# A mixture-of-experts stream written in a fixed engine order, and a hinted branch ahead of it

## The chip, the cores and the metric

The kernel runs on one core of a Trainium2 chip, in one launch. The metric is the device time of one execution in microseconds, as the median of several runs. TensorE multiplies (PE, its weight loads PEld), VectorE (DVE) and ScalarE (ACT) work beside it, SyncE (SP) holds the queue that issues the weight transfers, GpSimd (POOL) does little here.

## The reference, cut to what matters

The program is two transformer blocks on 256 tokens of width 1024, in float32: sliding-window attention, a feed-forward layer, a second attention, then a mixture of experts, and a second block of a recurrent and an attention mixer, memory attention and a feed-forward layer. The change is in the mixture of experts: each token goes to 2 of 8 experts.

```python
def _moe(x, router, w_gate, w_up, w_down):
    ...
    vals, ids = lax.top_k(logits, TOP_K)
    w = jax.nn.softmax(vals, axis=-1)
    gate = jnp.sum(jax.nn.one_hot(ids, N_EXPERTS, dtype=jnp.float32) * w[..., None], axis=1)
    out = jnp.zeros_like(xt)
    for e in range(N_EXPERTS):
        out = out + gate[:, e:e + 1].astype(xt.dtype) * _swiglu(xt, w_gate[e], w_up[e], w_down[e])
    return out.reshape(B, S, D)
```

An expert is `(silu(x @ w_gate) * (x @ w_up)) @ w_down` with a hidden width of 3584, so its three weights are 1024 x 3584, 1024 x 3584 and 3584 x 1024.

## The kernel before, in words

**Products.** Every float32 product is made of three: each operand is split into a high part in TensorE's short float32 and a low part, the rest. `gemm` (L260) multiplies high by high, high by low and low by high (L274 to L276) into one PSUM tile. Weights come in pieces of 256 rows by 512 columns, 512 KB each. `fetch` (L207) issues the transfer on SyncE's queue into one of 9 raw buffers (`NRAW`), `split_w` (L241) casts the piece to its high part on ScalarE (L256) and subtracts for the low part on VectorE (L257), into one of 5 pairs of split buffers (`NSPL`). A piece feeds six matmuls of 512 columns.

**Experts.** `moe` (L983) routes the tokens, gives each expert 128 slots and gathers its tokens into them by a product with a one-hot matrix (L1102); the tokens come two experts at a time. For each expert there are seven chunks of 512 hidden columns. A chunk is a gate product of 4 pieces (24 matmuls), the silu on ScalarE (L1162), an up product of 4 pieces, a multiplication on VectorE (L1170), and four transposes of the result on TensorE (L186), whose copy to a high part is ScalarE's (L189) and whose low part is VectorE's (L190). Then come two down products of 14 pieces, one for each half of the output columns; each is scaled by the gates (L1179, L1180) and scattered back to the tokens by a product with the transposed one-hot matrix (L1084, L1085) and added (L1087).

**Order.** The code is written product by product: the pieces of a product are loaded one by one where they are used, a gather is written where its part of the tokens is first read, and the transposes and the scatter right behind their product. That is not the order in which the engines run it. A scheduler takes the instructions when the program is built, ranks them by their place in the text and by its own estimate of when each is ready, and writes one fixed queue for each engine. What stands in a queue waits for what stands ahead of it. PSUM has four buffers for products and gathers (`mm`), two for transposes (`tr`), two for scatters (`at`).

**Slots from 128 on.** An expert can have more than 128 tokens. The largest count is read into a register on each engine (L1130), and a branch (L1131) goes past `moe_rest`, which would work on the slots from 128 on with a slower product. With these inputs the branch goes past it. Ahead of it 14 pieces are loaded (5 of them split, L1120), and the last four megabytes of weights of the last expert are parked in buffers of their own (L1153).

```python
full = nc.values_load(cnti[0:1, 0:1], min_val=0, max_val=T)
with tc.If(full > P):
    for e in range(NE):
        self.moe_rest(p, p2, onehots, scatter, e, Xh, Xl)
```

Of the kernel before, what the change touches and what calls it, by code (L numbers as in the profile page):

```python
# [8 lines left out]
F32 = mybir.dt.float32  # L9
# [89 lines left out]
class Net:  # L99
# [513 lines left out]
    def ffn_body(self, Wg, g0, Wu, u0, dff, Wd, emit, scale=None, beside=lambda p: None):  # L613
# [369 lines left out]
    def moe(self):  # L983
# [5 lines left out]
        with ExitStack() as c0:  # L989
# [103 lines left out]
            def gather(oh):  # L1093

                xg = [p.tile([P, KD, 2, P], F32R, tag=f"xg{n}", name="xg") for n in "hl"]

                def bring(k0):
                    for X, x in zip((Xh, Xl), xg):
                        ps = self.mm.tile([P, 2, 2, P], F32, tag="mm", name="mm")
                        for k in range(2):  # L1100
                            for tt in range(2):
                                nc.tensor.matmul(ps[:, k].rearrange("p a s -> p (a s)"), X[tt][:, (k0 + k) * P:(k0 + k + 1) * P],  # L1102
                                                 oh[:, tt].rearrange("p a s -> p (a s)"), start=tt == 0, stop=tt == 1)
# [5 lines left out]
                there = set()  # L1109
# [36 lines left out]
            for e0 in range(0, NE, 2):  # L1146
                oh, back = onehots((e0, e0 + 1), 0)
                brought = gather(oh)
                if e0 == 0:

                    last = [self.xp.tile([P, 4, 512], F32, tag="xh", name="parked"), *(p.tile([P, 4, 512], F32, name=f"parked{n}") for n in range(3))]
# [919 lines left out]
```

## Time and profile before

| what | us |
|---|---|
| median of 3 runs | 2371.4 (2370.0 to 2378.3) |
| the profiled execution, its own time | 2368.11 |
| its span, first to last instruction | 2366.3 |
| before the first gather of the experts | 601.76 |
| from there to the end of the last expert's last product | 1009.46 |
| from there to the end | 755.08 |
| TensorE busy, of the span | 2261.2 |
| VectorE, ScalarE busy | 1778.9, 1440.7 |

The profile is of one execution. Busy time of TensorE is modelled: a matmul is shown from its start to the end of its passage, which overlaps the next, so a stretch can be fully busy and still hold gaps between starts. An arrow in a row points from an instruction to what ended the idle time before it, or from a waiting engine to what it waited for. L12 is line 12 of the kernel; a name with q (PEq, SPq) is the engine's sequencer, which waits, branches and issues transfers.

### The profile page before, as it was taken

How to read it: one execution, taken by the hardware profiler on the slowest of the kernel's cores; microseconds unless marked ns; L12 is line 12 of the kernel's file. 1: busy time of each engine (PE TensorE's matmuls, PEld its weight loads, DVE VectorE, ACT ScalarE, POOL GpSimd, SP SyncE). 2: the span in 40 equal slices, each digit the busy share in tenths (PEclk: the TensorE clock that was granted, in tenths of full speed). 3: DMA queues.
4: the chain of work that ended last, by engine and by line, in shares of the span. 5: the costliest groups of instructions: out<-in, count | busy, mean ns of one | idle time of the engine just before them, and what ended most of it. 6: DMA issues, size and time to landing. Idle time of an engine off the chain costs nothing.

```text
span 2366.3 us, 35741 instructions
## 1 busy us (share of the span) xinstructions
PE 2261.2 (96%) x12969; PEld 1923.0 (81%) x12969; DVE 1778.9 (75%) x2849; ACT 1440.7 (61%) x2386; POOL 66.1 (3%) x78
## 2 busy tenths in 40 slices
PE   8999998999899999999999999996898999989998
PEld 6699977887787787778777877775898888988997
DVE  7765559766788988889888888887857765666664
ACT  5664436665677767777777777774553554455553
POOL 0000000000000000000000000001110110000000
PEclk9999999999899999999999999998998999999999
DMA  8366555434899999999999999994333213543761
GB/s 242 98 198 192 187 160 175 148 107 145 289 364 350 350 350 345 357 352 343 346 365 349 358 334 357 355 323 132 108 90 99 74 54 110 170 143 137 260 200 46
DMA packets 319711, 541.96 MB, mean 229 GB/s; under 512 B 21839, under 2 KB 95015, under 8 KB 319271
## 3 DMA queue, kind: packets, MB, share of 16 engines
q1 hardware_dynamic: 309680, 528.93, 66.6%
q10 hardware_dynamic: 9847, 10.67, 1.5%
q8 instruction: 104, 1.70, 0.3%
q14 instruction: 80, 0.66, 0.1%
HBM read 536.38 MB, written 3.15 MB: 228 GB/s over the span
## 4 chain that ended last, share of the span: by engine, by line
PE 65%; DVE 4%; issue 3%; ACT 1%; POOL 1%; DMA 0%; DVEq 0%; POOLq 0%; ACTq 0%
PE mm L275 15%; PE mm L276 15%; PE mm L274 15%; PE tr L186 2%; PE mm L688 1%; PE mm L318 1%; PE mm L689 1%; PE mm L687 1%; PE mm L319 1%; PE mm L317 1%; PE tr L1701 1%; DVE wl L254 1%; PE at L1712 1%; PE at L1715 1%; PE mm L1102 1%
## 5 line engine op out<-in xcount | busy, mean ns | idle before, releaser
L257 DVE TENSOR_TENSOR wl<-w,wh 128x1024 fp32r<-128x1024 f32 x755 | 884.4, 1219 | 171.9 <-ACT wh L256 166.9
L256 ACT CAST wh<-w 128x1024 fp32r<-128x1024 f32 x755 | 753.9, 1050 | 179.3 <-PE mm L276 114.2
L275 PE MATMUL mm<-wl,xg 128*128 128x512 f32 x896 | 364.8, 407 | 0.6
L276 PE MATMUL mm<-wh,xg 128*128 128x512 f32 x896 | 351.4, 392 | 0.0
L274 PE MATMUL mm<-wh,xg 128*128 128x512 f32 x896 | 349.7, 392 | 0.0
L253 ACT CAST wh<-w 128x512 fp32r<-128x512 f32 (+1 forms) x378 | 216.3, 616 | 135.5 <-PE mm L276 59.6
L254 DVE TENSOR_TENSOR wl<-w,wh 128x512 fp32r<-128x512 f32 (+1 forms) x378 | 247.1, 682 | 52.0 <-ACT wh L253 51.5
L275 PEld LDWEIGHTS mm<-wl,xg 128*128 128x128 f32 x896 | 168.4, 188 | 65.8 <-DVE wl L257 35.7
L274 PEld LDWEIGHTS mm<-wh,xg 128*128 128x128 f32 x896 | 168.2, 188 | 36.0
L276 PEld LDWEIGHTS mm<-wh,xg 128*128 128x128 f32 x896 | 168.8, 188 | 30.9 <-ACT xg L1105 1.4
L687 PE MATMUL mm<-xh,wh 128*128 128x256 f32 x672 | 187.4, 279 | 0.0
L689 PE MATMUL mm<-xl,wh 128*128 128x256 f32 x672 | 187.3, 279 | 0.0
L688 PE MATMUL mm<-xh,wl 128*128 128x256 f32 x672 | 187.3, 279 | 0.0
L275 PE MATMUL mm<-wl,h 128*128 128x512 f32 x448 | 177.1, 395 | 1.7 <-DVE wl L257 1.7
L276 PE MATMUL mm<-wh,h 128*128 128x512 f32 x448 | 174.6, 390 | 0.0
L274 PE MATMUL mm<-wh,h 128*128 128x512 f32 x448 | 174.5, 390 | 0.0
L687 PEld LDWEIGHTS mm<-xh,wh 128*128 128x128 f32 x672 | 127.4, 190 | 0.0
L688 PEld LDWEIGHTS mm<-xh,wl 128*128 128x128 f32 x672 | 126.3, 188 | 0.0
L689 PEld LDWEIGHTS mm<-xl,wh 128*128 128x128 f32 x672 | 126.2, 188 | 0.0
L275 PEld LDWEIGHTS mm<-wl,h 128*128 128x128 f32 x448 | 84.1, 188 | 22.8 <-DVE wl L257 6.1
L274 PEld LDWEIGHTS mm<-wh,h 128*128 128x128 f32 x448 | 84.1, 188 | 18.0 <-ACT wh L256 0.2
L276 PEld LDWEIGHTS mm<-wh,h 128*128 128x128 f32 x448 | 84.2, 188 | 16.6 <-issue 0.2
(615 smaller groups left out, 4466.7 us busy)
## 6 DMA issues: line engine op xcount, KB each, us to landing
w<-in_moe_w_gate_dram SPq DMA_DIRECT2D x224, 512.0 KB, 5.6
w<-in_moe_w_up_dram SPq DMA_DIRECT2D x224, 512.0 KB, 5.5
w<-in_moe_w_down_dram SPq DMA_DIRECT2D x216, 512.0 KB, 5.9
w<-in_w_in_dram SPq DMA_DIRECT2D x60, 512.0 KB, 3.8
w<-in_w_ffn_in_dram SPq DMA_DIRECT2D x40, 512.0 KB, 9.8
w<-in_ffn_w_gate_dram SPq DMA_DIRECT2D x28, 512.0 KB, 4.5
w<-in_ffn_w_up_dram SPq DMA_DIRECT2D x28, 512.0 KB, 4.4
w<-in_ffn_w_down_dram SPq DMA_DIRECT2D x28, 512.0 KB, 3.6
```

The source lines that it names most:

```text
L186: nc.tensor.transpose(ps[:, k, :], src[:, (k0 + k) * P:(k0 + k + 1) * P], self.idn)
L253: nc.scalar.copy(wh[:, ks, :n], w[:, ks, :n])
L254: nc.vector.tensor_sub(wl[:, ks, :n], w[:, ks, :n], f(wh[:, ks, :n]))
L256: nc.scalar.copy(wh[:, :nk, :n], w[:, :nk, :n])
L257: nc.vector.tensor_sub(wl[:, :nk, :n], w[:, :nk, :n], f(wh[:, :nk, :n]))
L274: nc.tensor.matmul(o, h, wh[:, k, :sn], start=k0 + k == 0, stop=False)
L275: nc.tensor.matmul(o, h, wl[:, k, :sn], start=False, stop=False)
L276: nc.tensor.matmul(o, l, wh[:, k, :sn], start=False, stop=k0 + k == nk - 1)
L317: nc.tensor.matmul(o, h, wh[:, k, :n], start=k0 + k == 0, stop=False)
L687: nc.tensor.matmul(o, wh[:, k, js], h, start=first and j % 2 == 0, stop=False)
L688: nc.tensor.matmul(o, wl[:, k, js], h, start=False, stop=False)
L689: nc.tensor.matmul(o, wh[:, k, js], l, start=False, stop=last and j % 2 == 1)
```

## The change

The experts' loop is written anew. The weight pieces of all experts form one list; `weights` keeps five of them split or on their way, so a piece's cast and subtraction are written four pieces ahead of its matmuls. `product` does one product and, after each piece, what has been put off to this point. `put_off(n, first, then)` puts TensorE's part of a side job n pieces later and its copies one piece after that: transposes (`hidden`) at 2, scatters (`spread_out`) at 2, and the gathers of the next pair, which are now begun ahead of the first down product of a pair's second expert, at 1 to 4. From there to the last down product, `manual_schedule` makes TensorE, ScalarE and VectorE issue in the order of the text; SyncE's queue stays the scheduler's.

The branch is turned round: its condition is `full <= P`, its taken arm a memset of a small tile, and `moe_rest` the arm that falls through. A hint that the branch is likely taken is placed ahead of the register load, for TensorE, VectorE and SyncE.

Five unused tiles of 64 to 192 bytes are put into the pools of the sliding-window attention, the feed-forward layers, the second attention, the mixer and the memory attention, which moves the tiles behind them by as much.

```diff
@@ swa, ffn_body, nsa, mixer, memory @@
             po = c0.enter_context(self.pool("heads", 1))
+            po.tile([P, 16], F32, name="lead")
...
             p = c.enter_context(self.pool("ffn", 1))
+            p.tile([P, 16], F32, name="lead")
...
             po = c0.enter_context(self.pool("heads", 1))
+            po.tile([P, 16], F32, name="lead")
...
             pm = c0.enter_context(self.pool("mixm", 1))
+            pm.tile([P, 32], F32, name="lead")
...
             ol = po.tile([P, 8, T], F32R, tag="ol", name="ol")
+            po.tile([P, 48], F32, name="tail")
...
@@ moe @@
                 def bring(k0):
-                    for X, x in zip((Xh, Xl), xg):
-                        ps = self.mm.tile([P, 2, 2, P], F32, tag="mm", name="mm")
...
-                        if X is Xl:
-                            nc.scalar.copy(x[:, k0:k0 + 2], ps)
-                        else:
-                            nc.vector.tensor_copy(x[:, k0:k0 + 2], ps)
...
-                def xs(i, k):
-                    if k not in there:
-                        there.update((k, k + 1))
-                        bring(k)
-                    return xg[0][:, k, i], xg[1][:, k, i]
-                return xs
+                    def first():
+                        ps = [self.mm.tile([P, 2, 2, P], F32, tag="mm", name="mm") for _ in range(2)]
+                        for X, o in zip((Xh, Xl), ps):
+                            for k in range(2):
+                                for tt in range(2):
+                                    nc.tensor.matmul(o[:, k].rearrange("p a s -> p (a s)"), X[tt][:, (k0 + k) * P:(k0 + k + 1) * P],
+                                                     oh[:, tt].rearrange("p a s -> p (a s)"), start=tt == 0, stop=tt == 1)
+                        return ps
+                    def then(ps):
+                        nc.vector.tensor_copy(xg[0][:, k0:k0 + 2], ps[0])
+                        nc.scalar.copy(xg[1][:, k0:k0 + 2], ps[1])
+                    return first, then
+                return xg, bring
...
+            tc.mark_branch_hint_location("rest", hint="LikelyTaken", engines=[mybir.EngineType.PE, mybir.EngineType.DVE, mybir.EngineType.SP])
             full = nc.values_load(cnti[0:1, 0:1], min_val=0, max_val=T)
-            with tc.If(full > P):
+            with tc.If(full <= P, preferred_fallthrough_block=False, label="rest") as few:
+                nc.vector.memset(cnt, 0.0)
+            with few.Else():
                 for e in range(NE):
                     self.moe_rest(p, p2, onehots, scatter, e, Xh, Xl)
...
-            for e0 in range(0, NE, 2):
+            pieces = []
+            for e in range(NE):
+                for j in range(0, F, 512):
+                    pieces += [(W[e], k * P, j, False) for W in (Wg, Wu) for k in range(0, KD, 2)]
+                pieces += [(Wd[e], k * P, c, e == NE - 1 and c > 0) for c in (0, 512) for k in range(0, NF, 2)]
+            pieces, held, later = iter(pieces), [], []
+            def weights():
+                while len(held) < NSPL:
+                    q = next(pieces, None)
+                    if q is None:
+                        break
+                    held.append(self.load_w(q[0], q[1], 2, q[2], 512, fine=q[3]))
+                return held.pop(0)
+            def product(nk, x):
+                ps = self.mm.tile([P, 512], F32, tag="mm", name="mm")
+                for k0 in range(0, nk, 2):
+                    wh, wl = weights()
+                    for k in range(2):
+                        h, l = x(k0 + k)
+                        nc.tensor.matmul(ps, h, wh[:, k], start=k0 + k == 0, stop=False)
+                        nc.tensor.matmul(ps, h, wl[:, k], start=False, stop=False)
+                        nc.tensor.matmul(ps, l, wh[:, k], start=False, stop=k0 + k == nk - 1)
+                    now = [w for w in later if w[0] == 1]
+                    later[:] = [[n - 1, w] for n, w in later if n > 1]
+                    for _, w in now:
+                        w()
+                return ps
+            def put_off(n, first, then):
+                got = []
+                later.append([n, lambda: got.append(first())])
+                later.append([n + 1, lambda: then(got[0])])
+            def pair(e0):
                 oh, back = onehots((e0, e0 + 1), 0)
-                brought = gather(oh)
...
-                    for j in range(F // 512):
-                        self.gemm(xs, Wg[e], KD, [(j * 512, 512)], emit_g, tts=(0,))
-                        if i == 0 and j == 0:
-                            oT, gs = back()
...
-                        def emit_u(_, c0, n, ps, tts=(0, 1)):
-                            nc.vector.tensor_mul(st["s"], st["s"], ps[0])
-                            hs[j] = [p.tile([P, 4, P], F32R, tag=f"h{n}", name="h", bufs=7) for n in "hl"]
-                            self.transpose_split(st["s"], 4, hs[j][0], hs[j][1])
-                        self.gemm(xs, Wu[e], KD, [(j * 512, 512)], emit_u, tts=(0,))
...
-                        nc.scalar.mul(yh, ps[0], gs[:, i:i + 1])
-                        nc.vector.scalar_tensor_tensor(yl, ps[0], gs[:, i:i + 1], f(yh), op0=OP.mult, op1=OP.subtract)
-                        scatter(yh, yl, oT, i, c0, e == NE - 1)
...
-                    for c0 in (0, 512):
-                        self.fine = e == NE - 1 and c0 > 0
-                        self.gemm(lambda k, tt: (hs[k // 4][0][:, k % 4], hs[k // 4][1][:, k % 4]), Wd[e], NF,
-                                  [(c0, 512)], emit_d, tts=(0,))
+                xg, bring = gather(oh)
+                for n, k0 in enumerate(range(0, KD, 2)):
+                    if e0:
+                        put_off(n + 1, *bring(k0))
+                    else:
+                        w = lambda a=bring(k0): a[1](a[0]())
+                        w() if n < 2 else later.append([n - 1, w])
+                return back, xg
+            def hidden(s, t):
+                def first():
+                    ps = self.tr.tile([P, 4, P], F32, tag="tr", name="tr")
+                    for k in range(4):
+                        nc.tensor.transpose(ps[:, k], s[:, k * P:(k + 1) * P], self.idn)
+                    return ps
+                def then(ps):
+                    nc.scalar.copy(t[0], ps)
+                    nc.vector.tensor_sub(t[1], ps, f(t[0]))
+                put_off(2, first, then)
+            def spread_out(yh, yl, oT, i, c0, stats):
+                def first():
+                    ps = [self.at.tile([P, 512], F32, tag="at", name="at") for _ in range(2)]
+                    for tt in range(2):
+                        nc.tensor.matmul(ps[tt], oT[:, i, tt], yh, start=True, stop=False)
+                        nc.tensor.matmul(ps[tt], oT[:, i, tt], yl, start=False, stop=True)
+                    return ps
+                def then(ps):
+                    for tt in range(2):
+                        y = acc[tt][:, c0:c0 + 512]
+                        nc.vector.tensor_add(y, y, ps[tt])
+                        if stats:
+                            nc.vector.bn_stats(self.st[tt][:, 0], y)
+                put_off(2, first, then)
+            nxt = pair(0)
+            last = [self.xp.tile([P, 4, 512], F32, tag="xh", name="parked"), *(p.tile([P, 4, 512], F32, name=f"parked{n}") for n in range(3))]
+            for n, t in enumerate(last):
+                self.park(Wd[NE - 1], (NF - 16 + n * 4) * P, 512, t)
+            order = c0.enter_context(ExitStack())
+            order.enter_context(tc.manual_schedule(engines={mybir.EngineType.PE, mybir.EngineType.Activation, mybir.EngineType.DVE}))
+            for e in range(NE):
+                i = e % 2
+                if i == 0:
+                    back, xg = nxt
+                x = lambda k: (xg[0][:, k, i], xg[1][:, k, i])
+                hs = []
+                for j in range(F // 512):
+                    ps = product(KD, x)
+                    if i == 0 and j == 0:
+                        oT, gs = back()
+                    t = p2.tile([P, 512], F32, tag="sil", name="sil")
+                    nc.scalar.activation(t, ps, AF.Silu)
+                    ps = product(KD, x)
+                    nc.vector.tensor_mul(t, t, ps)
+                    hs.append([p.tile([P, 4, P], F32R, tag=f"h{n}", name="h", bufs=7) for n in "hl"])
+                    hidden(t, hs[j])
+                if e == NE - 1:
+                    out["g"] = self.bcast(A["ln_gain"][1, 1], D, "gb", pool=p, tag="xgh")
+                    out["b"] = self.bcast(A["ln_bias"][1, 1], D, "bb", pool=p, tag="xgl")
+                for c in (0, 512):
+                    if i and c == 0 and e < NE - 1:
+                        nxt = pair(e + 1)
+                    if e == NE - 1 and c:
+                        order.close()
+                    ps = product(NF, lambda k: (hs[k // 4][0][:, k % 4], hs[k // 4][1][:, k % 4]))
+                    yh = p.tile([P, 512], F32R, tag="yh", name="yh")
+                    yl = p.tile([P, 512], F32R, tag="yl", name="yl")
+                    nc.scalar.mul(yh, ps, gs[:, i:i + 1])
+                    nc.vector.scalar_tensor_tensor(yl, ps, gs[:, i:i + 1], f(yh), op0=OP.mult, op1=OP.subtract)
+                    if e == NE - 1 and c:
+                        scatter(yh, yl, oT, i, c, True)
+                    else:
+                        spread_out(yh, yl, oT, i, c, e == NE - 1)
```

## Rows read from the trace of the kernel before

**Rows 1.** Window: length, busy (count) of PE PEld DVE ACT POOL, clock, DMA share, GB/s.

```profile
601.76:1611.22 1009.46, 1007.09 (x4496) 799.04 (x4496) 883.89 (x872) 735.26 (x826) 0.00 (x0) 1.00 0.97 344
```

**Rows 2.** Waits, 601.76 to 1611.22: engine, line waited for: us, times, longest.

```profile
ACT h L189 <- PE tr L186: 91.4, 51, 2.7
ACT sil L1162 <- PE mm L276: 69.5, 55, 2.4
...
PEld mm L275 <- DVE wl L257: 41.8, 134, 1.1
...
PE mm L1102 <- PEq L1131: 6.2, 1, 6.2
...
ACT wh L256 <- DMA w<-in_moe_w_down_dram: 3.3, 4, 2.2
```

**Rows 3.** Windows: five chunks of the first, six of the second expert.

```profile
627.14:683.88 56.74, 56.74 (x261) 46.90 (x260) 53.71 (x52) 45.52 (x49) 0.00 (x0) 1.00 1.04 381
736.21:807.55 71.34, 71.21 (x312) 54.36 (x311) 62.77 (x61) 52.55 (x60) 0.00 (x0) 1.00 0.99 350
```

**Rows 4.** Waits of TensorE's weight loads: in those six, then in those five chunks.

```profile
PEld mm L275 <- DVE wl L257: 5.3, 18, 0.6
PEld tr L186 <- DVE sil L1170: 1.8, 6, 0.3
...
PEld tr L186 <- DVE sil L1170: 0.3, 1, 0.3
```

**Rows 5.** Timeline of ScalarE in a fast chunk: start, length, instruction, count [idle before].

```profile
659.80 1.06 ACT L256 CAST wh<-w 128x1024 fp32r<-128x1024 f32 x1 [0.30 <-PE mm L276]
661.16 0.60 ACT L1162 ACTIVATE sil<-mm 128x512 f32<-128x512 f32 x1 [0.30 <-PE mm L276]
...
669.08 0.59 ACT L189 CAST h<-tr 128x512 fp32r<-128x512 f32 x1
```

**Rows 6.** Timeline of ScalarE in a slow chunk.

```profile
783.75 0.60 ACT L1162 ACTIVATE sil<-mm 128x512 f32<-128x512 f32 x1 [1.34 <-PE mm L276]
784.25 4.83 ACT L256 CAST wh<-w 128x1024 fp32r<-128x1024 f32 x5
790.86 0.59 ACT L189 CAST h<-tr 128x512 fp32r<-128x512 f32 x1 [1.78 <-PE tr L186]
```

**Rows 7.** Timeline of TensorE: four gather matmuls.

```profile
1111.11 0.63 PE L1102 MATMUL mm<-oh,Xl 128*128 128x256 f32 x4
```

**Rows 8.** Lines, 601.7 to 1612: shapes, count, busy us, mean ns, idle before.

```profile
L257 DVE TENSOR_TENSOR wl<-w,wh 128x1024 fp32r<-128x1024 f32 x653 | 759.5, 1218 | 53.1 <-ACT wh L256 51.8 <-DMA w<-in_moe_w_down_dram 0.3
...
L1170 DVE TENSOR_TENSOR sil<-sil,mm 128x512 f32<-128x512 f32 x56 | 38.4, 686 | 29.0 <-PE mm L276 28.6
...
L1107 DVE CAST xg<-mm 128x512 fp32r<-128x512 f32 x16 | 11.0, 685 | 7.1 <-PE mm L1102 7.1
```

**Rows 9.** Timeline before the branch.

```profile
595.40 0.17 PE L1026 MATMUL at<-selb,ub 128*128 128x8 bf16 x1
...
596.13 0.15 DVE L1032 CAST cnti<-cnt 128x1 int32<-128x1 f32 x1
```

**Rows 10.** Line L1131: count, ns min/median/max, first and last start in us.

```profile
L1131 SPq EVENT_SEMAPHORE  x8: 17/17/17, 601.4 to 602.0; - x8
...
L1131 PEldq COMPARE_BRANCH  x1: 4532/4532/4532, 596.9 to 596.9; - x1
...
L1131 DVEq EVENT_SEMAPHORE  x1: 21/21/21, 600.3 to 600.3; - x1
```

**Rows 11.** Windows: ahead of the branch and after it.

```profile
594.00:596.00 2.00, 0.27 (x5) 0.18 (x4) 1.79 (x13) 0.21 (x1) 0.00 (x0) 0.50 1.05 401
...
601.76:608.50 6.74, 6.74 (x29) 6.16 (x30) 1.94 (x3) 1.72 (x3) 0.00 (x0) 0.57 0.77 258
```

**Rows 12.** Windows: down products of the two feed-forward stages.

```profile
273.77:349.13 75.36, 75.36 (x325) 61.05 (x324) 36.82 (x38) 28.39 (x30) 0.43 (x1) 1.00 0.57 175
2298.58:2358.77 60.19, 60.19 (x265) 49.40 (x264) 28.14 (x29) 21.81 (x25) 0.57 (x1) 1.00 0.24 82
```

More of the change, by code (lines that the diff above doesn't have):

```diff
@@ L1097, in bring @@
                 def bring(k0):
-                    for X, x in zip((Xh, Xl), xg):
-                        ps = self.mm.tile([P, 2, 2, P], F32, tag="mm", name="mm")
[L1100 to L1103, printed above, removed]
-                        if X is Xl:
-                            nc.scalar.copy(x[:, k0:k0 + 2], ps)
-                        else:
-                            nc.vector.tensor_copy(x[:, k0:k0 + 2], ps)
-                there = set()
-                def xs(i, k):
-                    if k not in there:
-                        there.update((k, k + 1))
-                        bring(k)
-                    return xg[0][:, k, i], xg[1][:, k, i]
-                return xs
+                    def first():
[11 more added lines that the diff above has]
+                return xg, bring
             for n in range(NRAW + NSPL):
@@ L1144, in done @@
                     nc.vector.scalar_tensor_tensor(x, y, rs, out["b"][:, cs], op0=OP.mult, op1=OP.add)
-            for e0 in range(0, NE, 2):
-                oh, back = onehots((e0, e0 + 1), 0)
-                brought = gather(oh)
-                if e0 == 0:
-                    last = [self.xp.tile([P, 4, 512], F32, tag="xh", name="parked"), *(p.tile([P, 4, 512], F32, name=f"parked{n}") for n in range(3))]
-                    for n, t in enumerate(last):
-                        self.park(Wd[NE - 1], (NF - 16 + n * 4) * P, 512, t)
-                for i in range(2):
-                    e = e0 + i
-                    hs = {}
-                    xs = lambda k, tt: brought(i, k)
-                    st = {}
-                    def emit_g(_, c0, n, ps, tts=(0, 1)):
-                        st["s"] = p2.tile([P, 512], F32, tag="sil", name="sil")
-                        nc.scalar.activation(st["s"], ps[0], AF.Silu)
-                    for j in range(F // 512):
-                        self.gemm(xs, Wg[e], KD, [(j * 512, 512)], emit_g, tts=(0,))
-                        if i == 0 and j == 0:
-                            oT, gs = back()
-                        def emit_u(_, c0, n, ps, tts=(0, 1)):
-                            nc.vector.tensor_mul(st["s"], st["s"], ps[0])
-                            hs[j] = [p.tile([P, 4, P], F32R, tag=f"h{n}", name="h", bufs=7) for n in "hl"]
-                            self.transpose_split(st["s"], 4, hs[j][0], hs[j][1])
-                        self.gemm(xs, Wu[e], KD, [(j * 512, 512)], emit_u, tts=(0,))
-                    def emit_d(_, c0, n, ps, tts=(0, 1)):
-                        yh = p.tile([P, 512], F32R, tag="yh", name="yh")
-                        yl = p.tile([P, 512], F32R, tag="yl", name="yl")
-                        nc.scalar.mul(yh, ps[0], gs[:, i:i + 1])
-                        nc.vector.scalar_tensor_tensor(yl, ps[0], gs[:, i:i + 1], f(yh), op0=OP.mult, op1=OP.subtract)
-                        scatter(yh, yl, oT, i, c0, e == NE - 1)
-                    if e == NE - 1:
-                        out["g"] = self.bcast(A["ln_gain"][1, 1], D, "gb", pool=p, tag="xgh")
-                        out["b"] = self.bcast(A["ln_bias"][1, 1], D, "bb", pool=p, tag="xgl")
-                    for c0 in (0, 512):
-                        self.fine = e == NE - 1 and c0 > 0
-                        self.gemm(lambda k, tt: (hs[k // 4][0][:, k % 4], hs[k // 4][1][:, k % 4]), Wd[e], NF,
-                                  [(c0, 512)], emit_d, tts=(0,))
```

## The prediction

> **What bounds the kernel now.** I first cut the span at the start and the end of the experts' stage. That stage, from the first gather at 601.76 us to the last expert's last product at 1611.22, is 1009.46 us of the 2366.3, and TensorE counts as busy for 1007.09 of it at the full clock [rows 1]. So the engine does not stand idle there; whatever the change can win has to be hidden in the distance between matmuls. The view of waits over the same stretch shows who waits inside the queues: ScalarE 91.4 us for the transposes in 51 waits, 69.5 us for the gate product in 55, and TensorE's weight loads 41.8 us for the low half of a weight piece in 134 waits of about 0.3 us [rows 2]. Transfers end 3.3 us of waiting in all.
>
> A chunk is one gate and one up product of 512 hidden columns: 48 matmuls and 4 transposes, 52 records. Two stretches from silu to silu show two speeds [rows 3]: 56.74 us for five chunks of the first expert (11.35 each), 71.34 us for six of the second (11.89 each). In the slow six the weight loads waited 5.3 us for low halves (18 times, three per chunk) and others for the product; in the fast five they waited 0.3 us in all [rows 4]. ScalarE's timeline says why. In the fast chunk a cast goes ahead of the silu, each cast starts 0.30 us after the matmul that frees its buffer, and the copy of the transposes waits for nothing [rows 5]. In the slow one the silu stands ahead of a cast whose buffer is already free: ScalarE waits 1.34 us for the product, must then make five casts in a row (4.83 us), and waits 1.78 us at the copy, which also stands too early [rows 6]. The pieces reach TensorE late. It is the order in ScalarE's queue, not any engine's sum. The silu starts show 36 slow chunks out of 56 (6, 4, 6, 4, 6, 4, 6 in experts 1 to 7); the row of six stands for them.
>
> **The order, in chunks.** After the change each piece's cast is written four pieces ahead of its matmuls, the silu behind the cast of the fourth next piece, the transposes two pieces after their product and their copies three after. That is the fast chunk's order. A piece takes (11.35 - 0.4)/8 = 1.37 us of TensorE (four transposes at most 0.5 us, by the four 256-column gather matmuls in 0.63 [rows 7]). Cast 0.30 + 1.06, low half 1.22 [rows 5, 8]: ready 2.6 us after its buffer is free, needed 4 x 1.37 = 5.5 us after, so 2.9 us remain. Gain 36 x (11.89 - 11.35) = **19.4 us**; bounds 0 and 19.4.
>
> **The order, outside the chunks.** 36 slow chunks hold 108 of the 134 waits for low halves and 36 x 5.3/6 = 31.8 of the 41.8 us; 10 us lie in the down products and at the seams. In a slow chunk 5.3/6 + 0.3 = 1.2 us of weight-load waits cost 0.54 us, so 10 us cost about 4.6. I take **4.6**; bounds 0 and 10.
>
> **The gathers.** From the second pair on, one pair of PSUM buffers is filled after each of the first four pieces of the down product. Of four buffers the product holds one and the first gather two, so the second half of the second gather waits until VectorE has copied the first. That copy (0.68 us [rows 8]) stands behind the low half, which ends 1.2 us after TensorE's piece; TensorE meanwhile has 0.4 us of transposes and 0.47 of gather. It waits about 1.0 us, after which the queues have air. Queued behind it on TensorE is the whole stream. Three pairs: **loss 3.0 us**; bounds 0 and 9 (three gathers of each pair).
>
> **The branch.** TensorE's last matmul before it starts at 595.40 [rows 9]; its branch instruction lasts 4.53 us, VectorE's next instruction comes at 600.3, SyncE's at 601.4 [rows 10], and the first gather waited 6.2 us [rows 2]. A hint can start the fetch as early as TensorE passes it. If right behind the matmul at 595.40, the lead on the branch at 596.9 is 1.5 us; if earlier in the idle time, all 4.5 are saved. I take **3.0**; bounds 0 and 4.5. The first 6.74 us afterwards run at a granted clock of 0.57 [rows 11], mostly at the 1.2 GHz level, after TensorE had idled; this stretch moves with the start, so I cost it at nothing. The new arm's memset is one 128x1 instruction on VectorE, like the cast of 0.15 us [rows 9]; hidden behind the fetch, 0.15 us if not. SyncE's queue is not in the fixed order; it issues the same pieces and parked weights in the same sequence, and is bounded by the buffers that VectorE frees. The two transfers of the last gain and bias, issued by ScalarE, now stand behind the last up product: once, and covered by the 2.9 us that a cast has to spare. Other work before and after the stage stays the scheduler's. The page Runtime: NRT & Kernel Launch of the Trainium skill (Instruction fetch mechanics) says that prefetch is purely sequential and a taken branch out of the window must fetch first; the 4.53 us agree, and by that rule alone the 3.0 would go and the time be 2350.4.
>
> **The pads.** Five unused tiles of 64 to 192 bytes shift the operands of five other stages. The trace shows no such shift. Nearest are two down products of the same matmul form at different addresses: 75.36 us for 325 records and 60.19 for 265 [rows 12], 0.232 and 0.227 each. On some 800 matmuls (600 of the two down products, 192 of the two output projections) that is 4 us either way. I take **0**, the middle; 4 on both sides for the range.
>
> **Sum.** 19.4 + 4.6 + 3.0 - 3.0 = 24.0 us. The profiled execution took 2368.1 us (span and 1.8 around it), 3.3 under the median of 2371.4; I take the difference from the median: **2347.4 us**.
>
> **Rivals.** (1) The transfers become the bound. Eight pieces are 4.19 MB; the slow chunks draw 350 GB/s at a share of 0.99 [rows 3]. If that were the ceiling, chunks could not shrink, nothing would be gained outside them, and branch and gathers cancel: 2371. Against it: the fast chunks drew 381 GB/s over 56.74 us [rows 3], and 401 were seen before the branch [rows 11]; the fast chunk needs 370. Chance 0.10. The Trainium skill, SBUF — State Buffer (A bandwidth-pool intuition that's wrong), gives about 358 GB/s from HBM to one core; an estimate from that page is 11.72 us per chunk, a gain of 6 us instead of 19.4. The 381 differ from it, and the measurement decides.
>
> (2) VectorE falls behind: the slower side. In the fast stretch it was busy 53.71 of 56.74 us [rows 3], 95%. The transposes stand fixed two pieces, 2.73 us, after the up product; the product's multiplication (0.69 us) runs behind a low half that ends 1.2 us after, so 0.8 us are left. If two more low halves stand ahead of it (2.4 us), TensorE waits 1.6 us with the whole stream behind it, in 56 chunks: 90 us, 2437. It outweighs the gains once the wait passes 24.0/56 = 0.43 us, that is, from 1.2 us of backlog. Against it: the fast chunks have the same sum and no such wait. Chance 0.08.
>
> (3) Half: the silu's wait goes, but 95% on VectorE leaves small waits for low halves at half of today's price: 2359 to 2360. Chance 0.10.
>
> (4) The hint does not do what it says: the branch keeps its 4.53 us, 2350.4. That lies inside the forecast's own range and has three chances in ten of it.
>
> **How the numbers follow.** The forecast has 0.72. All gains at their bounds, with the pads, are 19.4 + 10 + 4.5 + 4 = 38: low 2333. Upwards I reach past the half case to 2364, which leaves out (1) and (2), 0.18. About 0.5%, or 12 us, is what a measurement of this kernel can tell from no change, so faster begins under 2359.5: 0.72 and half of (3), 0.77; same: (1) and the other half, 0.15; slower: 0.08.
>
> **What would show it.** Right: silu to silu 11.3 to 11.4 us in all 56 chunks; ScalarE's waits for transposes near nothing; the weight loads' 41.8 us under 10; the stage near 988 us from first gather to last product, its transfers at about 352 GB/s; TensorE's branch near 1.5 us and the first gather near 598.8; a wait of about 1 us in the gather after the down product's second piece. Wrong: chunks still at 11.9 with casts waiting for transfers (1), with transposes waiting for the multiplication (2), a 4.5 us branch (4), or a stage before 590 or after the experts that moved by more than 4 us (pads).

## The result, and the profile after

The median is 2337.13 us (2333.16 to 2347.70, four runs) against 2374.85 of the kernel before on the same chip (four runs). The ratio is 0.9849 with a 95% interval of 0.9808 to 0.9891: faster by 1.5%, 26 to 46 us by the interval. The profiled execution took 2333.16 us, 1.8 of them outside its span of 2331.4; before it was 2368.11 and 2366.3. The 34.9 us between the spans lie here:

| stretch | before | after | change |
|---|---|---|---|
| start to the end of the selection that feeds the routing matmuls (L1018, now L1021) | 595.24 | 593.43 | -1.8 |
| from there to the first gather | 6.52 | 2.62 | -3.9 |
| first gather to the start of the last product's scaling (L1179, now L1265) | 1009.46 | 984.33 | -25.1 |
| from there to the end | 755.07 | 750.99 | -4.1 |

The windows of the profile after, with the columns of [rows 1]: the stage, six chunks of the second expert as in [rows 3], and the stage's first stretch.

```profile
596.05:1581.00 984.95, 981.52 (x4496) 813.00 (x4496) 903.97 (x876) 771.18 (x828) 0.00 (x0) 1.00 0.98 353
729.06:797.24 68.18, 68.18 (x313) 56.40 (x312) 63.93 (x62) 55.80 (x60) 0.00 (x0) 1.00 1.01 366
596.05:601.70 5.65, 5.65 (x21) 5.20 (x22) 1.38 (x2) 2.03 (x3) 0.00 (x0) 0.50 0.31 88
```

TensorE counts as just as busy as before, in 25 us less. The six chunks that took 71.34 us [rows 3] take 68.18, 11.36 each. The views of waits over the stage, against [rows 2]:

```profile
ACT wh L256 <- PE mm L1175: 166.8, 490, 1.2
DVE wl L257 <- ACT wh L256: 43.8, 72, 1.3
ACT sil L1249 <- PE mm L1175: 17.2, 55, 0.4
...
PEld mm L1106 <- DVE oh L1060: 4.6, 6, 1.2
...
PE mm L1106 <- DVE oh L1060: 2.4, 3, 0.8
PEld mm L1106 <- ACTq L1132: 2.4, 1, 2.4
PE mm L1106 <- DVE cnt L1133: 2.3, 1, 2.3
...
ACT wh L253 <- DMA w<-in_moe_w_down_dram: 1.0, 2, 0.8
```

TensorE's weight loads no longer wait for low halves (41.8 us before), and ScalarE no longer waits at the copy of the transposes (91.4 before). ScalarE's idle time now lies in front of its casts: it waits for TensorE to free a buffer, and no weight load waits for what comes of it. ScalarE's timeline of one chunk, against [rows 6]:

```profile
763.16 0.60 ACT L1249 ACTIVATE sil<-mm 128x512 f32<-128x512 f32 x1 [0.33 <-PE mm L1175]
763.65 1.99 ACT L256 CAST wh<-w 128x1024 fp32r<-128x1024 f32 x2
765.88 1.06 ACT L256 CAST wh<-w 128x1024 fp32r<-128x1024 f32 x1 [0.24 <-PE mm L1175]
...
771.32 1.05 ACT L256 CAST wh<-w 128x1024 fp32r<-128x1024 f32 x1 [0.31 <-PE mm L1175]
772.28 0.58 ACT L1209 CAST h<-tr 128x512 fp32r<-128x512 f32 x1
773.15 1.06 ACT L256 CAST wh<-w 128x1024 fp32r<-128x1024 f32 x1 [0.30 <-PE mm L1175]
774.51 0.60 ACT L1249 ACTIVATE sil<-mm 128x512 f32<-128x512 f32 x1 [0.30 <-PE mm L1175]
```

The silu waits 0.3 us instead of 1.34, two casts follow without a gap instead of five, then each cast follows its buffer. The branch's rows (count, ns, starts), against [rows 10]:

```profile
L1132 PEldq COMPARE_BRANCH  x1: 392/392/392, 595.1 to 595.1; - x1
```

The hint itself stands in the trace at the head of the three engines' queues, on TensorE's at 0.8 us:

```profile
L2150 PEldq BRANCH_PREFETCH_HINT  x1: 50/50/50, 0.8 to 0.8; - x1
```

The gathers of the second pair, timelines of VectorE and TensorE:

```profile
804.15 1.11 DVE L1060 TENSOR_SCALAR oh<-slots,pos,sel 128x128 fp32r<-128x128 f32 x4
804.80 1.13 PE L1106 MATMUL mm<-oh,Xh 128*128 128x256 f32 x4 [0.80 <-DVE oh L1060]
805.17 2.35 DVE L257 TENSOR_TENSOR wl<-w,wh 128x1024 fp32r<-128x1024 f32 x2
...
807.44 0.68 DVE L1111 CAST xg<-mm 128x512 fp32r<-128x512 f32 x1
...
808.00 0.72 PE L1106 MATMUL mm<-oh,Xh 128*128 128x256 f32 x4
...
808.56 0.63 PE L1106 MATMUL mm<-oh,Xl 128*128 128x256 f32 x4
```

The first gather waits 0.80 us for the one-hot matrix. At the second, the low tokens' matmuls begin 0.56 us after the high ones, where 0.48 is usual. VectorE's copy, whose buffer they take, had ended at 808.12, 0.44 us before them, and no row shows a wait for it: it cost 0.1 us at most.

### The profile page after: what moved, and what is told of

Its sections match the earlier page's. It is cut to its first block, busy times and chain, and to the rows that moved or that the text cites. A ratio compares the mean times of both kernels' runs of the same rounds, so it can differ in the third digit from the quotient of the medians.

```text
span 2331.4 us, 35736 instructions
## 1 busy us (share of the span) xinstructions
PE 2230.7 (96%) x12969; PEld 1934.5 (83%) x12969; DVE 1798.3 (77%) x2850; ACT 1475.4 (63%) x2386; POOL 66.5 (3%) x78
## 4 chain that ended last, share of the span: by engine, by line
PE 87%; DVE 6%; issue 3%; ACT 2%; DMA 1%; POOL 1%; SPq 0%; DVEq 0%; POOLq 0%; ACTq 0%
PE mm L1173 13%; PE mm L1175 13%; PE mm L1174 13%; PE mm L276 5%; PE mm L274 5%; PE mm L275 5%; PE mm L690 3%; PE mm L689 3%; PE mm L691 3%; PE mm L1907 2%; PE mm L318 1%; PE mm L319 1%; PE mm L317 1%; DVE wl L254 1%; PE sc L909 1%
## 5 line engine op out<-in xcount | busy, mean ns | idle before, releaser
L257 DVE TENSOR_TENSOR wl<-w,wh 128x1024 fp32r<-128x1024 f32 x755 | 905.8, 1222 | 185.8 <-ACT wh L256 156.5
L256 ACT CAST wh<-w 128x1024 fp32r<-128x1024 f32 x755 | 788.0, 1053 | 302.1 <-PE mm L1175 166.8
L1174 PE MATMUL mm<-wl,xg 128*128 128x512 f32 x896 | 349.4, 390 | 0.0
L254 DVE TENSOR_TENSOR wl<-w,wh 128x512 fp32r<-128x512 f32 (+1 forms) x378 | 247.8, 683 | 53.1 <-ACT wh L253 52.3
```

The source lines that it names most:

```text
L254: nc.vector.tensor_sub(wl[:, ks, :n], w[:, ks, :n], f(wh[:, ks, :n]))
L256: nc.scalar.copy(wh[:, :nk, :n], w[:, :nk, :n])
L257: nc.vector.tensor_sub(wl[:, :nk, :n], w[:, :nk, :n], f(wh[:, :nk, :n]))
L1174: nc.tensor.matmul(ps, h, wl[:, k], start=False, stop=False)
```

## The experiments

In kernels that don't differ in the stage it repeats to about a microsecond (983.35 to 984.33 in the changed kernel, 1, 3, 8 and 12). The stretch ahead of it ranges over 18 us, the one behind it over ten, so the stage, not the ratio, tells the kernels apart. One profile each, in us; "to gather" is from the selection's end to the first gather, the stage as in the table above, the ratio to the kernel before with its interval (kernel 8 has a single run):

| kernel | silu to silu | ahead | to gather | stage | behind | ratio |
|---|---|---|---|---|---|---|
| before | 11.37 and 11.89 | 595.24 | 6.52 | 1009.46 | 755.07 | |
| after | 11.37 | 593.43 | 2.62 | 984.33 | 750.99 | 0.9849 (0.9808 to 0.9891) |
| 1 no pads | 11.37 | 593.95 | 2.62 | 983.84 | 755.52 | 0.9858 (0.9828 to 0.9889) |
| 2 pads alone | 11.37 and 11.91 | 588.19 | 7.72 | 1009.07 | 754.30 | 0.9981 (0.9953 to 1.0009) |
| 3 hint out | 11.37 | 605.70 | 7.11 | 983.35 | 757.24 | 0.9885 (0.9840 to 0.9930) |
| 4 free order | 12.01 | 606.10 | 2.64 | 1017.05 | 755.34 | 0.9980 (0.9961 to 0.9999) |
| 5 three pieces held | 11.63 | 590.45 | 2.62 | 996.64 | 751.46 | 0.9904 (0.9869 to 0.9939) |
| 6 four pieces held | 11.37 | 593.78 | 2.62 | 983.25 | 751.37 | 0.9859 (0.9815 to 0.9903) |
| 7 transposes at 1 piece | 11.85 | 595.27 | 2.62 | 1006.60 | 748.05 | 0.9955 (0.9934 to 0.9976) |
| 8 hint for TensorE alone | 11.37 | 594.30 | 7.12 | 983.90 | 749.94 | |
| 9 three held, transposes at 3 matmuls | 12.35 | 606.11 | 2.62 | 1031.74 | 757.67 | 1.0039 (1.0007 to 1.0071) |
| 10 three held, transposes at 1 piece | 11.67 | 593.63 | 2.62 | 997.35 | 750.90 | 0.9891 (0.9840 to 0.9941) |
| 11 fourteen unread matmuls | 11.37 | 593.85 | 3.95 | 981.71 | 755.48 | 0.9829 (0.9771 to 0.9887) |
| 12 nine unread matmuls | 11.37 | 605.67 | 3.00 | 983.68 | 751.33 | 0.9872 (0.9839 to 0.9905) |

**1 and 2, the pads.** Taken out of the changed kernel, and put alone into the kernel before.

```diff
-            po.tile([P, 16], F32, name="lead")
-            p.tile([P, 16], F32, name="lead")
-            po.tile([P, 16], F32, name="lead")
-            pm.tile([P, 32], F32, name="lead")
-            po.tile([P, 48], F32, name="tail")
```

> The changed kernel without the five unused tiles, all else as it is. Theory P (the pads are real): what was gained outside the stage and the branch, 1.8 us before the branch and 4.1 after the experts, is theirs, so the span goes from 2331.4 to about 2337.3, and the high and low products of the first feed-forward layer's down product go back from 0.226 to 0.233 us from one start to the next (336 matmuls, 2.2 us). Theory N (noise): the 5.9 us are the spread of single executions; the span stays within 2 us of 2331.4 and the pitch stays at 0.226. Either way 11.36 us from silu to silu and a first gather 2.5 us behind the last routing matmul.

> The kernel before with the five unused tiles and nothing else of the change. Theory P: 5.9 us less, a span near 2360.4 instead of 2366.3, with 1.8 of it ahead of the branch and 4.1 after the experts; the pitch of the down product falls from 0.233 to 0.226. Theory N: span 2365 to 2368. Either way silu to silu stays at 11.89 in 36 chunks and the branch at 4.5 us.

Both theories are half right. The distances from each matmul of the two feed-forward layers' down products to TensorE's next start add up to 79.08 and 60.20 us before and to 77.70 and 60.22 without the pads; in all twelve kernels that have the pads they are 77.00 to 77.04 and 59.61 to 59.66. So 0.7 to 2.1 us in the first and 0.6 in the second are the pads' own, 1.3 to 2.7 in all. The other 3 to 5 of the 5.9 us are not shown to be theirs: with the pads the stretch behind the stage took 748.05 to 757.67, without them 755.07 and 755.52, and the ratio of kernel 2 has 1 in its interval.

**3 and 8, the hint.** Out, and for TensorE alone.

```diff
-            tc.mark_branch_hint_location("rest", hint="LikelyTaken", engines=[mybir.EngineType.PE, mybir.EngineType.DVE, mybir.EngineType.SP])
+            tc.mark_branch_hint_location("rest", hint="LikelyTaken", engines=[mybir.EngineType.PE])
```

> The changed kernel without the hint, with the branch still turned round. Theory H (the hint does it): TensorE's branch goes back from 0.39 to about 4.5 us, the first gather from 2.5 to 6.4 us behind the last routing matmul, VectorE's memset comes about 3 us later, and the span grows by 3.9 to about 2335.3. Rival T (turning the branch round does it, since the taken arm is now the short one): the branch stays at 0.4 us and the span at 2331.4.

> The changed kernel with the hint for TensorE alone. Theory V: VectorE's own fetch then shows (its first instruction came 3.3 us behind its branch in the kernel before, 3.5 us without any hint), the first gather waits for VectorE's memset, and it comes about 5.5 us behind the last routing matmul instead of 2.5; TensorE's branch stays at 0.4 us. Rival: the gather needs TensorE's fetch only and stays at 2.5 us.

The branch instruction's row without the hint; the same with the hint for TensorE alone; and VectorE's and TensorE's next instructions in the timeline of that kernel:

```profile
L1131 PEldq COMPARE_BRANCH  x1: 5092/5092/5092, 607.4 to 607.4; - x1
```

```profile
L1132 PEldq COMPARE_BRANCH  x1: 397/397/397, 596.0 to 596.0; - x1
```

```profile
601.22 0.06 DVE L1133 MEMSET cnt<- 128x1 f32 x1 [4.96 <-issue]
...
601.42 1.19 PE L1106 MATMUL mm<-oh,Xh 128*128 128x256 f32 x4 [6.79 <-DVE cnt L1133]
```

Theory H holds, and theory V in kind. Turning the branch round gives nothing by itself: without the hint it takes 5.09 us (4.53 in the kernel before, 5.69 in kernel 2). With the hint for TensorE alone its branch is down to 0.40 us and nothing is gained: the gather waits for VectorE, which comes 5.0 us late, and the 7.12 us are those without any hint (7.11). Theory V had put VectorE's delay at 3.3 to 3.5 us and the gather 5.5 us behind the last routing matmul; it came 7.0 behind. So a hint for TensorE alone is worth nothing. A hint for VectorE alone, or for TensorE and VectorE without SyncE, was not run. Kernels without a hint took 6.52 to 7.72 us to the first gather, those with it for three engines 2.62 (2.64 in kernel 4; more only with the unread matmuls of 11 and 12): the hint is worth 3.9 to 5.1 us, and 3.9 against the profile of the kernel before. It stands some 594 us ahead of the branch, and the branch still comes down to 0.39.

**4, the order left to the scheduler.**

```diff
-            order.enter_context(tc.manual_schedule(engines={mybir.EngineType.PE, mybir.EngineType.Activation, mybir.EngineType.DVE}))
```

> The changed kernel with the same text but without the fixed order: the scheduler ranks the instructions again. In its queue for ScalarE the silu stands two casts earlier than in the changed kernel in 49 of 56 chunks, as it did in the 36 slow chunks of the kernel before (with one cast earlier, in three chunks of before, the next silu came after 11.37 us). Theory S (two casts too early costs 0.53 us per chunk): silu to silu 11.37 in the first expert and 11.89 from the second on, 49 x 0.53 = 26 us in the chunks, span 2357 to 2363. Rival G (it is the new text, transposes and gathers put off, that makes the chunks fast): 11.36 everywhere, span 2331 to 2334.

Theory S, and more: 11.37 in the first expert, 12.01 from the second on, 1017.05 us, 7.6 more than the kernel before. The new text is worth nothing in the stage; its fixed order is worth 32.7 us. The scheduler moved three things: the silu two casts ahead, the transposes from twelve matmuls behind the up product to seven, and their copy on ScalarE four casts ahead (five casts behind the silu instead of seven). In the kernel before the transposes stood four behind the up product in the slow chunks and seven to nine in the fast ones, which I had not looked at; the copy stood in the slow ones as early as here. The waits over the stage of kernel 4, and TensorE's weight loads in one chunk:

```profile
ACT h L1209 <- PE tr L1205: 111.0, 50, 2.7
...
PEld mm L1174 <- DVE wl L257: 45.0, 115, 1.0
```

```profile
788.85 0.19 PEld L1174 LDWEIGHTS mm<-wl,xg 128*128 128x128 f32 x1 [0.39 <-DVE wl L257]
...
793.18 0.19 PEld L1174 LDWEIGHTS mm<-wl,xg 128*128 128x128 f32 x1 [0.34 <-DVE wl L257]
...
797.17 0.58 PEld L1205 LDWEIGHTS tr<-idn,sil 128*128 128x128 f32 x4
```

Two low halves are late in each chunk: one in the third piece behind the silu (793.18), one in the fourth piece behind the up product (788.85), after ScalarE has stood at the copy for some 2.4 us. The transposes wait for nothing here. So 0.64 us per chunk can be lost without any wait of TensorE for VectorE's multiplication.

**5 and 6, the silu's place.** Fewer pieces are held, so each cast is written later and the silu stands two casts, or one, earlier, and the copy of the transposes with it; TensorE's order stays as it is. The diff is that of kernel 5; kernel 6 has 1 in place of 2.

```diff
-                while len(held) < NSPL:
+                while len(held) < NSPL - 2:
```

> The changed kernel with three pieces held instead of five, the order fixed as before: each cast and low half is written two pieces ahead of its matmuls instead of four, so every silu stands two casts earlier in ScalarE's queue, as in the 36 slow chunks of the kernel before, and nothing else moves. Theory S (the silu's place among the casts): after the silu the cast for the third next piece comes first; it is ready 0.30 + 0.60 + 1.06 + 1.22 = 3.2 us behind the end of the gate product and TensorE wants it after two pieces, 2.7 us: 0.45 us or more lost in each chunk, silu to silu 11.8 to 12.0 in all 56, the stage from first gather to last product's end 1010 to 1020 us instead of 984. Rival G (transposes and gathers put off make the chunks fast, not the casts): 11.36, 984 to 986.

> The same with four pieces held: every silu stands one cast earlier. Theory S: the cast for the fourth next piece follows the silu, ready 3.2 us behind the product and wanted after three pieces, 4.1 us: nothing is lost, silu to silu 11.37, the stage 984 to 986 us. If the loss grew evenly with the lead (rival L), it would be half of what two casts cost, 11.6 to 11.7 and a stage near 998.

The waits with three held, from 610 to 1590 us:

```profile
ACT h L1209 <- PE tr L1205: 86.8, 55, 2.1
ACT sil L1249 <- PE mm L1175: 72.1, 55, 1.9
...
PEld mm L1174 <- DVE wl L257: 19.1, 53, 0.4
```

ScalarE's two waits of [rows 2] are back, and so are the low halves', but once per chunk and not three times [rows 4], and a chunk costs 0.26 us, not 0.53. The expectation's "nothing else moves" is not exact, since the copy moves too. But the one wait lies where theory S put it, in the third piece behind a silu that starts at 738.97 us, and none lies behind the copy:

```profile
741.82 0.19 PEld L1174 LDWEIGHTS mm<-wl,xg 128*128 128x128 f32 x1 [0.36 <-DVE wl L257]
```

One cast early costs nothing, as theory S had it: the loss is a threshold, not a slope. So the silu's place is a cause and about half of the slow chunk, not all of it.

**7, 9 and 10, the transposes' place.** One piece behind the up product in the changed kernel; with three pieces held, three matmuls behind, and one piece behind. Their copies move along. The diff is that of kernel 7.

```diff
-                put_off(2, first, then)
+                put_off(1, first, then)
```

> The changed kernel with the transposes one piece behind the up product instead of two (their copies two instead of three). This prices the rival in which TensorE waits for VectorE's multiplication. In the changed kernel the multiplication of one chunk ended at 862.12 us and the transposes began at 862.87 (their weights' load); one piece earlier they would begin near 861.7, so TensorE waits about 0.45 us in each chunk: silu to silu 11.8, 56 x 0.45 = 25 us, the stage near 1009 us instead of 984. If VectorE gets the multiplication done earlier by itself, less: 11.36 and 984.

> The changed kernel with three pieces held and the transposes moved to three matmuls behind the up product (their copies to the end of that piece). That is the slow chunk of the kernel before in both respects: there each slow chunk had its silu two casts early and its transposes four matmuls behind the up product, each fast one seven to nine. Theory B (both make the slow chunk): the casts alone cost 0.26 us, the transposes' early place the other 0.27, silu to silu 11.85 to 12.0, the stage 1007 to 1015 us. Rival C (the casts alone, and the missing 0.27 lies elsewhere): 11.63, stage 997.

> The same with the transposes one piece (six matmuls) behind the up product. With five pieces held this place cost 0.48 us per chunk, since the multiplication stood behind low halves written four pieces ahead. Theory B: with three held it stands behind two low halves fewer, starts about 0.3 us after the up product, ends 1.0 us after it, and the transposes come 1.4 us after it, so they wait for nothing: 11.63 as with three held alone, stage near 997 us. Rival A (the two losses add): 11.63 + 0.48 = 12.1, stage near 1022.

The waits of kernel 7, from 610 to 1590 us, and of kernel 9, from 615:

```profile
PEld tr L1205 <- DVE sil L1251: 39.5, 56, 0.7
...
PE tr L1205 <- DVE sil L1251: 15.9, 56, 0.3
```

```profile
PEld tr L1210 <- DVE sil L1256: 50.0, 55, 1.0
...
PE tr L1210 <- DVE sil L1256: 26.6, 52, 0.5
...
PEld mm L1174 <- DVE wl L257: 18.7, 52, 0.4
```

Kernel 7 gives 0.48 per chunk, where 0.45 was expected: TensorE waits in every chunk for VectorE's multiplication. Kernel 10 gives 11.67, close to theory B: with the casts written later the multiplication stands further ahead, and the same place costs 0.04 (the transposes do wait, 13.0 us in 53 times, but most of it is hidden). Kernel 9 overshoots, 12.35 against 11.85 to 12.0: the early place is a cost, but the kernel before paid less. It is not quite the slow chunk of before: its transposes stand three matmuls behind the up product, not four, and VectorE's timelines differ, first of kernel 9, then of the kernel before:

```profile
749.72 4.64 DVE L257 TENSOR_TENSOR wl<-w,wh 128x1024 fp32r<-128x1024 f32 x4 [0.43 <-ACT wh L256]
754.27 0.68 DVE L1256 TENSOR_TENSOR sil<-sil,mm 128x512 f32<-128x512 f32 x1
```

```profile
749.65 3.50 DVE L257 TENSOR_TENSOR wl<-w,wh 128x1024 fp32r<-128x1024 f32 x3 [0.81 <-ACT wh L256]
753.77 0.69 DVE L1170 TENSOR_TENSOR sil<-sil,mm 128x512 f32<-128x512 f32 x1 [0.63 <-PE mm L276]
```

In kernel 9 the multiplication comes straight from a fourth low half; in the kernel before there were three, and VectorE already stood waiting for the product. That this makes the difference is argued from the timelines, not run. Nor was a kernel run that moves the copy and leaves the transposes. So transposes too early are shown as a cost, and what part of the slow chunk of before was theirs is not.

**11 and 12, the clock at the start.** Matmuls whose result nobody reads, in TensorE's idle time around the routing; ten ahead and four behind, then nine. The nine are written as four and five, but one of the five was issued ahead as well (605.23 below), so five run ahead and four behind. The diff is that of kernel 11.

```diff
+            busy = self.at.tile([P, 512], F32, tag="at", name="busy")
+            for n in range(10):
+                nc.tensor.matmul(busy, Xh[0][:, :P], Xh[0][:, :512], start=True, stop=True)
...
+            for n in range(4):
+                nc.tensor.matmul(busy, Xh[0][:, :P], Xh[0][:, :512], start=True, stop=True)
```

> The changed kernel with fourteen matmuls whose result nobody reads, ten ahead of the routing matmuls and four behind them, in the time in which TensorE had idled 6.2 and 2.3 us before the first gather. The first 5.7 us of the stage ran at the 1.2 GHz level of the granted clock; from the first gather to the first silu took 13.0 to 13.6 us. Theory W (TensorE's idling ahead of the branch set that clock): the first gathers run at 2.4 GHz, first gather to first silu about 10.5 us, 2.5 to 3 us less in all, too little for the times of the runs but plain in the profile. Rival: the clock does not follow these matmuls, 13.0 us as before; or the added matmuls hold up the routing by as much as they save.

> The changed kernel with nine unread matmuls instead of fourteen, five ahead of the routing matmuls. With ten ahead, the last of them ended at 595.46 us, while the routing's input had been ready at 593.85: 1.4 us of the 2.1 to 2.6 that the faster start gave went into that wait. Theory W: with five, the routing matmuls follow their input within 0.3 us; first gather 2.4 us behind the last routing matmul, and from there to the first silu 10.9 us if the shorter activity lifts the clock as well, 13.0 if it doesn't. With both, from the routing's input being ready to the first silu some 13.6 us, against 16.2 in the changed kernel and 14.9 with ten. Rival: the clock follows the longer activity only, 13.0 and no gain.

TensorE's timeline and a window with ten ahead, then the timeline with five:

```profile
591.54 3.92 PE L1026 MATMUL busy<-Xh 128*128 128x512 f32 x10 [3.78 <-DVE nm L1006]
...
597.81 0.71 PE L1111 MATMUL mm<-oh,Xh 128*128 128x256 f32 x4 [1.20 <-DVE cnt L1138]
598.35 0.63 PE L1111 MATMUL mm<-oh,Xl 128*128 128x256 f32 x4
```

```profile
595.80:602.00 6.20, 5.00 (x34) 4.28 (x33) 2.83 (x10) 2.46 (x3) 0.00 (x0) 1.00 0.83 299
```

```profile
603.36 2.08 PE L1026 MATMUL busy<-Xh 128*128 128x512 f32 x4 [3.71 <-DVE nm L1006]
605.23 0.63 PE L1034 MATMUL busy<-Xh 128*128 128x512 f32 x1
...
605.87 2.05 PE L1034 MATMUL busy<-Xh 128*128 128x512 f32 x4
608.67 1.19 PE L1111 MATMUL mm<-oh,Xh 128*128 128x256 f32 x4 [0.76 <-DVE cnt L1138]
609.67 1.05 PE L1111 MATMUL mm<-oh,Xl 128*128 128x256 f32 x4
```

Theory W holds for ten: the granted clock is 1.00 where it was 0.50, four gather matmuls take 0.63 us instead of 1.05, and the first silu comes 10.92 us after the first gather instead of 12.6 to 13.6 in the changed kernel and kernels 1 to 10 that have its text. But the ten hold up the routing matmuls by 1.45 us, so from the selection's end to the last scaling it is 985.67 us against 986.95 (986.46 without pads): about 1 us, less than the runs can tell. Five did not lift the clock and gained nothing. No version beats the changed kernel by more than is measurable.

## Why the prediction was right, and where its sizes were off

The forecast was 2347.4 in a range of 2333 to 2364; the runs gave 2337.1, near the fast end. The profiled spans differ by 34.9 us where 24.0 had been forecast: 29.0 in the stage and at the branch, and 5.9 where 0 had been put. The time is inside the range because its fast end takes each term at its bound; the mechanism held, and the largest term had the right size.

**The order, in chunks (19.4).** Measured 36 x 0.53 = 19.1 us, with all chunks at 11.35 to 11.37 except the first two (11.44, 11.31) and the first of each later pair (12.7 instead of 11.14, since the one-hots' transposes and the gate matmuls, 1.35 us of TensorE's own work, now stand there). The size was right, the reason shown in part: the silu two casts early is 0.26 of the 0.53 (kernel 5). The other 0.27 goes with the transposes, and how it splits stays open. In each slow chunk TensorE waited 0.30 us for VectorE's multiplication at the transposes: that is the 1.8 us in six chunks of [rows 4], which I counted into the price without asking where it came from. It also waited for a low half in the second and in the fourth piece behind the up product (0.22 and 0.28), behind VectorE's multiplication and ScalarE's early copy. Kernels 7 and 9 show that early transposes cost, and kernel 4, whose transposes wait for nothing, loses 0.64. Nor is the new order quite the fast chunk's, as I had said: there the transposes stood seven to nine matmuls behind, here twelve.

**Outside the chunks (4.6) and the gathers (-3.0).** Together 1.6 predicted, 25.1 - 19.1 = 6.0 measured. The gathers lost 3 x 0.80 = 2.4 us, so 8.4 is left for the other part, a remainder in which the 12.7 us chunks count, and no row of its own. Its clearest piece is the stretch from the last silu of a pair's first expert to the first silu of its second, which holds no gather: 52.3 to 52.9 us before, 51.3 after, 6.0 us in four. Kernel 4 has 52.2 to 52.9 there, so it is the fixed order that gains it. The term that I mis-sized is then the rate of 0.54 us lost per 1.2 us of waits, taken from a chunk: 8.4 of the 10 us came back. That the waits themselves were dearer there is argued. The loss at the gathers was nearly the right size in the wrong place, by luck. I had VectorE's copy at the second gather 1.0 us late; it was 0.1 at most, in part because the first gather itself takes TensorE 1 us while the low halves run, which I left out. The wait is at the first gather, for the one-hots, which VectorE makes behind the multiplication. Making them earlier was not tried.

**The branch (3.0).** Measured 3.9. The step that failed is the hint's place: not right behind the last matmul, but at the head of the queues, so TensorE's branch fell from 4.53 to 0.39 us and not to 1.5. And the term looked at TensorE alone: by kernel 8 VectorE's 5.0 us would have taken its place. The Trainium skill (Runtime: NRT & Kernel Launch, Instruction fetch mechanics) has the prefetch as purely sequential; the 5.09 us without the hint agree, and the 0.39 us with it are what the rule doesn't cover. Rival 4 is refuted.

**The pads (0).** 1.3 to 2.7 us are shown, in the very matmuls that [rows 12] named as the nearest; what else of the 5.9 is theirs stays open.

**The rivals.** (1) The transfers were no ceiling: six chunks ran at 366 GB/s, and ScalarE waited 1.0 us for them in the stage. The Trainium skill's figure of about 358 GB/s (SBUF — State Buffer, A bandwidth-pool intuition that's wrong) is a stack's 716 divided by two cores; this kernel runs on one core and drew more, and the measurement decides. (2) VectorE did not fall behind, but the margin was what I had said: I put 0.8 us between the multiplication's end and the transposes; it was 862.87 - 862.12 = 0.75, and one piece less costs 22 us (kernel 7). That is the price that the put-off of 2 avoids. (3) No low half was late, so half of the gain was not lost.

**What would show it.** As forecast: chunks at 11.3 to 11.4; no waits for transposes; low halves' waits 41.8 to none; 353 GB/s (352 forecast). Off: the stage 984.3, not 988; the first gather at 596.05, not 598.8; the stretch behind the experts 4.1 us shorter, just past the 4 that I had set, though the spread there is ten.

## What to carry to other kernels

When an engine is fully busy and its neighbours wait inside their queues, write down for each queue how far ahead of its use each step stands: here a silu two casts early, with the transposes and their copy early as well, cost 0.53 us in each of 36 chunks, 19 us in a stage in which TensorE counted as busy throughout, and a silu one cast early cost nothing. Price a wait with the queue's distance as well as the engine's load, and vary the distance to see where the threshold lies. A branch that all engines pass was here as late as the last engine that the next step waited for: hinting TensorE alone gained nothing, since VectorE came 5.0 us late. So give the hint to every engine that the next step waits for.

## What the runs showed of the hardware that I had not expected

A hint some 594 us ahead of its branch, at the head of the program, still took TensorE's branch from 4.5 to 5.7 us down to 0.4. With a tile of 64 bytes ahead of the first feed-forward layer's tiles, the starts of its 512-column down matmuls lay 0.227 us apart in all twelve kernels, and 0.233 and 0.229 in the two without (medians of 336); why those two differ from each other is open. And the first attention stage has two speeds, which don't go with the kernel, since the instructions there are the same: windows of TensorE there, first of the changed kernel, then of kernel 3, with the clock as the third number from the end:

```profile
50.00:90.00 40.00, 39.31 (x206) 28.21 (x205) 31.05 (x90) 31.97 (x111) 0.00 (x0) 1.00 0.19 60
```

```profile
50.00:90.00 40.00, 39.31 (x157) 26.52 (x157) 24.43 (x77) 24.30 (x92) 0.00 (x0) 0.70 0.13 42
```

At a mean clock of 0.70 the same engine is as busy and does a quarter less. The four profiles with 605 us and more ahead of the stage (kernels 3, 4, 9 and 12) lost some 10 us there, a quarter of the 40. What sets the speed is open. It is one reason why the spans of single executions can't be compared, and stages can.
